# A transformer kernel on Trainium2: ScalarE's and VectorE's order set by hand around the norm ahead of the FFN, transposes over four PSUM banks, eight operand sums moved

## The chip, the cores and the metric

The kernel runs on one core of one Trainium2 chip. The metric is the device time of one execution in microseconds (us). Three runs of the kernel before were timed; the trace is of a further execution, taken with the hardware profiler. TensorE (PE) does matmuls and transposes, ScalarE (ACT) casts and activations, VectorE (DVE) sums and products, GpSimd (POOL) some sums and the stores; SyncE (SP) issues the loads.

## What is computed

Two transformer blocks in a row, on 1024 tokens of width 1024, in float32. The first is attention and a mixture of experts. The second is a gated delta rule and a band attention side by side, an output product with w_out2, and an FFN with a causal convolution. Cut to what stands around the change, with the second block's names:

```python
x = rmsnorm(x1, norm_final)            # end of the first block
x = x + mix @ w_out                    # "w_out2" in the kernel
h = rmsnorm_2(x, norm_ffn_w)           # the norm ahead of the FFN
u = causal_dwconv(h @ w_up, conv_ffn_w) + conv_ffn_b
gate, up = jnp.split(u, 2, axis=-1)
x = x + (jax.nn.silu(gate) * up) @ w_down
```

## The kernel before

**Products in halves.** Every float32 operand of a product is split into a high and a low part (`split`, L53 to L62: a cast on ACT, L59, and a subtraction on VectorE, L62), and a product is three matmuls per k-tile (`acc3`): high by high, high by low, low by high. Names ending in h or hi, and l or lo, are these parts.

**w_out2.** `phase2_wout` computes mix @ w_out2 and adds it to x, which it holds as `xs`, eight row blocks of 128 tokens (they come in by SP's queue and are first multiplied by the first block's norm, L1713). Two halves `hf` of four row blocks each; in each half four loads `n`, each of 256 columns of w_out2. `load` (by `load_w`) brings a load as four pieces: a transfer of 256 KB into a raw tile `waraw`, a cast to `wahi`, a subtraction to `walo`. There are two raw tiles and six pairs wahi and walo. For each of the four row blocks 24 matmuls of 256 columns (8 k-tiles by 3) go to one PSUM bank of two (`pa(0, 2)`, tiles t0 and t1), and VectorE adds the bank to xs (L1779, "the xs sum"). The matmuls' left operands are `mh` and `ml`, parts of mix.

**The posts.** The first four row blocks are complete after half 0. Their norm lies in half 1: behind loads 0 and 1 two `post(t)` each. A post is a Square on ACT with a sum (L1719), the reciprocal root (L69 on VectorE, the root L100 on ACT, L101 to L104 on VectorE), the scaling (L1721) into `XN[t]`, and two `put`s: four transposes on PE (L44) to a bank, then the split into B11 (first 512 columns of the row block) and B21 (the others), the right operands of the FFN's products. `put` takes the banks t2 and t3 in turn (`pa(2, 4)`).

**The last four row blocks** are prepared behind load 2 (`early_post`: a Square of the first half, and L1742, the product of 768 columns with the norm's weights) and finished behind load 3 (`late_post`, L1746 to L1753): the Square of the other half, the product of 256 columns, the root's chain, a scaling on ACT, and two subtractions, L1752 and L1753, which make the operands of the FFN's `t1` and `t2` products: the FFN is done with Strassen-Winograd's seven products per block, and B11, B21, t1, t2, t3, t4 and 22 are their right operands.

**The first two FFN steps.** E holds four pieces of w_up2, loaded and split ahead (`early`, raw tile waraw as well). A loop of four does `prod` (48 matmuls) with E, then puts t1 and t2 of row block i, and then two sums on GpSimd (L1800 and L1801) that make the operands of t3 and t4. `phase2_ffn` then goes on with the pairs j; ahead of its first products it runs `late`, the puts of t3, t4 and 22, one between each two products.

**What sets the order.** PE's order is written out by hand from the last w_out2 load on (`tc.manual_schedule(engines={PE})`, entered at L1771): PE takes its instructions as they are written. Elsewhere, and on the other engines throughout, the framework's scheduler places each instruction on its engine's queue by its own account of when it can start, so that the written order and the queue's order differ. Each engine works its queue in order, and waits by semaphore for the others.

## Time and profile before

| | |
|---|---|
| median of three runs | 2887.88 us (2882.08 to 2892.51) |
| profiled execution | 2887.97 us, span 2886.2 us |
| instructions | 37138 |
| PE busy | 2671.0 us, 93% of the span |
| VectorE busy | 1840.4 us, 64% |
| ACT busy | 1241.2 us, 43% |
| GpSimd busy | 1105.5 us, 38% |
| TensorE's granted clock, mean | 0.965 |

The span runs from the first to the last instruction of the profiled execution. A row of the busy time by stretch says between which two times of the span it lies, how long that is, how long each engine worked in it (and in how many instructions, in brackets), what clock TensorE was granted (PEclk, 1.00 is full speed), what share of the time the DMA engines were busy and what they moved. A row of waits says which instruction waited for which, how long in sum, how often, and the longest. The product with w_out2 begins at about 2075 us, its last load ends near 2181, and from 2240 on only the FFN's products run on PE.

### The profile page before, as it was taken

What the parts mean: (1) busy time and instruction counts of PE and PEld (TensorE: products, weight loads), DVE (VectorE), ACT (ScalarE), POOL (GpSimd) and SP (SyncE); (2) the same over time, 40 slices, a digit from 0 to 9 for tenths busy, and PEclk for the clock granted to TensorE, in tenths of its full rate; (3) what the DMA queues carried; (4) which work ended last, traced back from release to release, by engine and by line L of the source; (5) the groups of instructions that cost most, each with busy time, mean ns of one, the idle gap of its engine ahead of it and who ended that gap; (6) DMA issues with size and microseconds to landing.
All of it is one profiled execution on the core that took longest, in us unless ns stands there. A gap on an engine that the chain in (4) does not pass through costs nothing.

```text
span 2886.2 us, 37138 instructions
## 1 busy us (share of the span) xinstructions
PE 2671.0 (93%) x13916; PEld 2143.9 (74%) x13916; DVE 1840.4 (64%) x2725; ACT 1241.2 (43%) x2032; POOL 1105.5 (38%) x950
## 2 busy tenths in 40 slices
PE   6999998999948999699999899999997999999998
PEld 4786665555836777588889788877896888888886
DVE  3655557784687998756437334375656998886354
ACT  4545554454325676543322223454234444443343
POOL 1103437887344888412121232040004766662000
PEclk8998999999978999899999999999999999999999
DMA  7113310001567999612453544312532122225452
GB/s 226 42 40 122 118 37 1 1 23 34 175 223 246 373 373 370 196 37 88 155 180 111 189 144 139 116 45 88 164 114 103 73 88 82 87 78 200 145 179 99
DMA packets 175956, 382.83 MB, mean 133 GB/s; under 512 B 18664, under 2 KB 84200, under 8 KB 170656
## 3 DMA queue, kind: packets, MB, share of 16 engines
q1 hardware_dynamic: 153056, 298.45, 30.6%
q0 software_dynamic: 22720, 82.02, 8.5%
q8 instruction: 109, 1.79, 0.3%
q14 instruction: 71, 0.58, 0.1%
HBM read 311.19 MB, written 69.22 MB: 132 GB/s over the span
## 4 chain that ended last, share of the span: by engine, by line
PE 50%; DVE 4%; issue 1%; DMA 1%; ACT 1%; POOL 0%; SPq 0%; DVEq 0%; ACTq 0%; POOLq 0%
PE t L41 25%; PE big L41 22%; PE t L44 2%; DVE Rb L1396 1%; DVE bP L1593 0%; DVE Rt L1395 0%; DVE xs L1713 0%; DMA xs<-xacc 0%; ACT bPT L1611 0%; DVE Al L62 0%; DVE mm L1589 0%; DVE walo L62 0%; DMA waraw<-in_w_up 0%; DMA out<-y 0%; DVE rst L102 0%
## 5 line engine op out<-in xcount | busy, mean ns | idle before, releaser
L62 DVE TENSOR_TENSOR mlo<-mraw,mhi 128x2048 fp32r<-128x2048 f32 x63 | 220.2, 3521 | 10.1 <-ACT mhi L59 10.0
L41 PE MATMUL big<-hhi,whi 128*128 128x512 f32 x656 | 210.5, 400 | 0.0
L41 PE MATMUL big<-hlo,whi 128*128 128x512 f32 x656 | 208.5, 396 | 0.0
L41 PE MATMUL big<-hhi,wlo 128*128 128x512 f32 x656 | 207.5, 395 | 0.0
L59 ACT CAST mhi<-mraw 128x2048 fp32r<-128x2048 f32 x96 | 181.5, 1913 | 56.0 <-PE big L41 30.3
L62 DVE TENSOR_TENSOR Al<-raw,Ah 128x512 fp32r<-128x512 f32 x150 | 115.6, 772 | 129.4 <-ACT Ah L59 127.6
L62 POOL TENSOR_TENSOR mlo<-mraw,mhi 128x2048 fp32r<-128x2048 f32 x33 | 164.9, 5002 | 76.0 <-ACT mhi L59 75.4
L59 ACT CAST Ah<-raw 128x512 fp32r<-128x512 f32 x150 | 92.7, 621 | 217.5 <-PE t L41 215.4
L812 POOL TENSOR_TENSOR acc<-acc,P 128x512 f32<-128x512 f32 x128 | 167.9, 1338 | 36.3 <-ACT P L805 35.7
L62 DVE TENSOR_TENSOR wlo<-wraw,whi 128x512 fp32r<-128x512 f32 (+5 forms) x124 | 78.7, 644 | 122.7 <-ACT whi L59 121.2
L805 ACT ACTIVATE P<-t 128x512 f32<-128x512 f32 x160 | 94.6, 597 | 120.2 <-PE t L41 116.6
L41 PEld LDWEIGHTS big<-hlo,whi 128*128 128x128 f32 x656 | 122.8, 189 | 26.3
L41 PEld LDWEIGHTS big<-hhi,wlo 128*128 128x128 f32 x656 | 122.8, 189 | 26.1
L41 PEld LDWEIGHTS big<-hhi,whi 128*128 128x128 f32 x656 | 121.0, 189 | 23.6
L59 ACT CAST whi<-wraw 128x512 fp32r<-128x512 f32 (+5 forms) x124 | 69.8, 573 | 139.9 <-PE big L41 118.1
L1841 DVE SCALAR_TENSOR_TENSOR cacc<-ml,cols,cacc 128x1023 f32<-128x1023 f32 x88 | 124.1, 1411 | 9.1 <-ACT cacc L1839 8.4
L700 DVE TENSOR_REDUCE mm<-big 128x1 f32<-128x640 f32 x128 | 101.7, 815 | 28.6 <-PE big L41 28.2
L62 DVE TENSOR_TENSOR Al<-S,Ah 128x512 fp32r<-128x512 f32 x88 | 118.3, 1347 | 2.6 <-ACT Ah L59 2.4
L41 PE MATMUL t<-whi,hlo 128*128 128x344 f32 (+2 forms) x320 | 107.6, 336 | 2.9 <-DVE hlo L62 2.5
L1897 POOL TENSOR_TENSOR cacc<-cacc 128x1024 f32<-128x1024 f32 x22 | 61.0, 2773 | 126.9 <-ACT Ah L59 123.7
L41 PE MATMUL t<-whi,hhi 128*128 128x344 f32 (+2 forms) x320 | 108.3, 338 | 0.8 <-ACT z L1198 0.3
L41 PE MATMUL t<-mlo,xh 128*128 128x512 f32 x256 | 101.7, 397 | 6.1 <-POOL mlo L62 3.3
(701 smaller groups left out, 7878.2 us busy)
## 6 DMA issues: line engine op xcount, KB each, us to landing
mraw<-in_w_gate SPq DMA_DIRECT2D x32, 1024.0 KB, 14.5
mraw<-in_w_up SPq DMA_DIRECT2D x32, 1024.0 KB, 13.3
mraw<-in_w_down SPq DMA_DIRECT2D x32, 1024.0 KB, 9.5
wmod<-in_w_mod SPq DMA_DIRECT2D x48, 512.0 KB, 6.2
raw<-in_w_up SPq DMA_DIRECT2D x22, 1024.0 KB, 4.8
raw<-in_w_down SPq DMA_DIRECT2D x22, 1024.0 KB, 5.1
wraw<-in_w2a SPq DMA_DIRECT2D x72, 256.0 KB, 2.8
zd<-cacc POOLq DMA_DIRECT2D x22, 512.0 KB, 3.0
```

The costliest lines, as they stand in the source:

```text
L41: self.nc.tensor.matmul(out, lhsT, rhs, start=start, stop=stop)
L44: self.nc.tensor.transpose(out, in_, self.ident[:n, :n])
L59: nc.scalar.copy(hi, src)
L62: (nc.vector if lo_eng == "dve" else nc.gpsimd).tensor_sub(lo, src, hi.bitcast(F32))
L700: nc.vector.reduce_max(r[:, a * 2 + 1 - e:a * 2 + 2 - e], ps.rearrange("p (a b) -> p a b", a=2)[:, :, :320], axis=AX.XY)
L805: nc.scalar.activation(P, ps, AF.Exp, scale=self.sc_mla)
L812: eng.tensor_add(u["acc"][e], u["acc"][e], P)
L1396: nc.vector.reduce_sum(R[:, j, j + 1:], tmp[:, :n * n].rearrange("p (m i) -> p i m", i=n), axis=AX.X)
L1841: nc.vector.scalar_tensor_tensor(t[:, tap:], x[:, :1024 - tap], self.col("conv_f", (2 - tap) * 44 + m), t[:, tap:], op0=ALU.mult, op1=ALU.add)
L1897: nc.gpsimd.tensor_mul(tg, tg, tu)
```

## The change

1. `others`: ACT's and VectorE's order is set by hand too, by a second `manual_schedule`, made beside PE's, entered at the last load of half 1 and left behind the loop of the first four FFN products.
2. `late_post` is cut into `squares(t)`, `scaled(t)` and `sums(t)`, which are written one row block apart: behind row block t's matmuls stand its squares, the scaling of t - 1 and the sums of t - 2. The scaling of row block 7 and the sums of 6 and 7 stand behind the first and second FFN product.
3. `banks`: in the loop of four the puts take the banks t0 to t3 in turn; afterwards t2 and t3 again.
4. The pieces E[1, b] are loaded and split behind the loop's entry, and no longer ahead of load 3's matmuls.
5. The four sums for t3 go from GpSimd to VectorE (`third`), those for t4 stay on GpSimd (`fourth`); both are written ahead of their puts, behind the first weights' sums in `phase2_ffn`.

```diff
--- before.py
+++ after.py
@@ -1722,7 +1722,7 @@
             nc.gpsimd.dma_start(self.xsd[t * 128:(t + 1) * 128, :], xs[t])
 
         def put(op, i, src):
-            ps = self.pa(2, 4)
+            ps = self.pa(*banks[0])
             for f in range(4):
                 self.tp(ps[:, f * 128:(f + 1) * 128], src[:, f * 128:(f + 1) * 128])
             s = slice(i * 128, (i + 1) * 128)
@@ -1734,6 +1734,7 @@
             put("21", t, XN[t][:, 512:])
 
         SS = {}
+        banks = [(2, 4)]
 
         def early_post(t):
 
@@ -1741,16 +1742,21 @@
             nc.scalar.activation(T2[t], xs[t][:, :512], AF.Square, accum_out=SS[t][:, 0:1])
             nc.vector.tensor_mul(XN[t][:, :768], xs[t][:, :768], nm[:, :768])
 
-        def late_post(t):
-            x, y, t2, ss = XN[t], XN[t - 4], T2[t], SS[t]
-            nc.scalar.activation(t2, xs[t][:, 512:], AF.Square, accum_out=ss[:, 1:2])
-            nc.vector.tensor_mul(x[:, 768:], xs[t][:, 768:], nm[:, 768:])
+        def squares(t):
+            nc.vector.tensor_mul(XN[t][:, 768:], xs[t][:, 768:], nm[:, 768:])
+            nc.scalar.activation(T2[t], xs[t][:, 512:], AF.Square, accum_out=SS[t][:, 1:2])
             nc.gpsimd.dma_start(self.xsd[t * 128:(t + 1) * 128, :], xs[t])
+
+        def scaled(t):
+            ss = SS[t]
             nc.vector.tensor_add(ss[:, 0:1], ss[:, 0:1], ss[:, 1:2])
             rs = self.rsqrt(ss[:, 0:1], 1.0 / 1024)
-            nc.scalar.activation(x, x, AF.Copy, scale=rs)
+            nc.scalar.activation(XN[t], XN[t], AF.Copy, scale=rs)
+
+        def sums(t):
+            x, y = XN[t], XN[t - 4]
             nc.vector.tensor_sub(y[:, :512], x[:, :512], y[:, :512])
-            nc.vector.tensor_sub(t2, x[:, 512:], y[:, :512])
+            nc.vector.tensor_sub(T2[t], x[:, 512:], y[:, :512])
 
         def early(j, b):
             raw = wo.tile([128, 512], F32, name="waraw", bufs=2)
@@ -1762,12 +1768,14 @@
         def load(src):
             return self.load_w(wo, src, 256, ks=8, kb=2, tag="wa", rawbufs=2, bufs=6)
         order = self.order = tc.manual_schedule(engines={mybir.EngineType.PE})
+        others = tc.manual_schedule(engines={mybir.EngineType.Activation, mybir.EngineType.DVE})
         for hf in range(2):
             for n in range(4):
                 W = load(I["w_out2"][n])
                 if hf and n == 3:
-                    E = {(j, b): early(j, b) for j in range(2) for b in range(2)}
+                    E = {(0, b): early(0, b) for b in range(2)}
                     order.__enter__()
+                    others.__enter__()
                 for i in range(4):
                     t = hf * 4 + i
                     ps = self.pa(0, 2)
@@ -1780,7 +1788,11 @@
                     if hf and n == 2:
                         early_post(t)
                     if hf and n == 3:
-                        late_post(t)
+                        squares(t)
+                        if i:
+                            scaled(t - 1)
+                        if i > 1:
+                            sums(t - 2)
                 if hf == 1 and n < 2:
                     post(2 * n)
                     post(2 * n + 1)
@@ -1792,22 +1804,38 @@
                 T2 = {4 + i: v[i // 2][:, i % 2 * 512:i % 2 * 512 + 512] for i in range(4)}
         ab = [self.big() for _ in range(2)]
         self.ff0 = [[], []]
+        banks[0] = (0, 4)
         for i in range(4):
             j, b = i // 2, i % 2
+            if i == 0:
+                E.update({(1, b): early(1, b) for b in range(2)})
             self.ff0[j].append(self.prod(ab[j][:, b * 512:(b + 1) * 512], E[j, b], B["21" if b else "11"]))
+            if i == 0:
+                scaled(7)
+                sums(6)
+            if i == 1:
+                sums(7)
             put("t1", i, XN[i][:, :512])
             put("t2", i, T2[4 + i])
-            nc.gpsimd.tensor_sub(XN[4 + i][:, :512], XN[4 + i][:, 512:], XN[4 + i][:, :512])
-            nc.gpsimd.tensor_sub(XN[i][:, 512:], XN[i][:, 512:], T2[4 + i])
+        others.__exit__(None, None, None)
+        banks[0] = (2, 4)
 
         def late(op, slot, srcs):
             v = self.mp.tile([128, 8, 512], F32R, name=slot)
             B[op] = v[:, :4], v[:, 4:]
             for i, src in enumerate(srcs):
                 put(op, i, src)
-        self.late = [lambda: late("t3", "mh1", [XN[4 + i][:, :512] for i in range(4)]),
-                     lambda: late("t4", "ml1", [XN[i][:, 512:] for i in range(4)]),
-                     lambda: late("22", "mh0", [XN[4 + i][:, 512:] for i in range(4)])]
+
+        def third():
+            for i in range(4):
+                nc.vector.tensor_sub(XN[4 + i][:, :512], XN[4 + i][:, 512:], XN[4 + i][:, :512])
+            late("t3", "mh1", [XN[4 + i][:, :512] for i in range(4)])
+
+        def fourth():
+            for i in range(4):
+                nc.gpsimd.tensor_sub(XN[i][:, 512:], XN[i][:, 512:], T2[4 + i])
+            late("t4", "ml1", [XN[i][:, 512:] for i in range(4)])
+        self.late = [third, fourth, lambda: late("22", "mh0", [XN[4 + i][:, 512:] for i in range(4)])]
 
     def phase2_ffn(self):
         nc, tc, I = self.nc, self.tc, self.I
```

In the built program PE's order is the same in both. The other engines' orders differ in the following places. In the rows, xs_17065 to xs_17072 are the row blocks 0 to 7, mh_17604 (before) and mh_17606 (after) is XN[0] to XN[3], ml_17605 and ml_17607 XN[4] to XN[7], t_17607 and t_17609 T2; a t with another number is a PSUM bank.

VectorE in half 0, around the xs sums of load 2, before:

```order
L1779 TENSOR_TENSOR xs_17065<-xs_17065,t_17372 128x256
L62 TENSOR_TENSOR walo<-waraw,wahi 128x512
L1779 TENSOR_TENSOR xs_17066<-xs_17066,t_17398 128x256
L1779 TENSOR_TENSOR xs_17067<-xs_17067,t_17424 128x256
L62 TENSOR_TENSOR walo<-waraw,wahi 128x512 x2
L1779 TENSOR_TENSOR xs_17068<-xs_17068,t_17450 128x256
L62 TENSOR_TENSOR walo<-waraw,wahi 128x512
```

VectorE at the same place in half 0, after:

```order
L62 TENSOR_TENSOR walo<-waraw,wahi 128x512 x4
L1787 TENSOR_TENSOR xs_17065<-xs_17065,t_17374 128x256
L1787 TENSOR_TENSOR xs_17066<-xs_17066,t_17400 128x256
L1787 TENSOR_TENSOR xs_17067<-xs_17067,t_17426 128x256
L1787 TENSOR_TENSOR xs_17068<-xs_17068,t_17452 128x256
L62 TENSOR_TENSOR walo<-waraw,wahi 128x512 x4
```

The four subtractions of a load (L62 on walo), which stood between the xs sums of the load ahead of it, now stand in one piece behind all four of these sums; it is so from load 2 of half 0 on.

VectorE in half 1, behind the last xs sum of half 0, at the first two posts (rsv, rsy and rst are tiles of the reciprocal root), before:

```order
L1779 TENSOR_TENSOR xs_17068<-xs_17068,t_17578 128x256
L69 TENSOR_SCALAR rsv<-ssx 128x1 x2
L1779 TENSOR_TENSOR xs_17069<-xs_17069,t_17632 128x256
L101 RECIPROCAL rsy<-rst 128x1 x2
L102 SCALAR_TENSOR_TENSOR rst<-rsy 128x1 x2
L103 TENSOR_TENSOR rst<-rst,rsv 128x1 x2
L104 SCALAR_TENSOR_TENSOR rsy<-rst,rsy 128x1 x2
L62 TENSOR_TENSOR walo<-waraw,wahi 128x512
L1721 SCALAR_TENSOR_TENSOR mh_17604<-xs_17065,rsy,row_16536 128x1024
L1779 TENSOR_TENSOR xs_17070<-xs_17070,t_17658 128x256
L1721 SCALAR_TENSOR_TENSOR mh_17604<-xs_17066,rsy,row_16536 128x1024
```

VectorE at the same two posts, after, from the last xs sum of half 1's load 0 on:

```order
L1787 TENSOR_TENSOR xs_17072<-xs_17072,t_17712 128x256
L69 TENSOR_SCALAR rsv<-ssx 128x1
L101 RECIPROCAL rsy<-rst 128x1
L102 SCALAR_TENSOR_TENSOR rst<-rsy 128x1
L103 TENSOR_TENSOR rst<-rst,rsv 128x1
L104 SCALAR_TENSOR_TENSOR rsy<-rst,rsy 128x1
L1721 SCALAR_TENSOR_TENSOR mh_17606<-xs_17065,rsy,row_16536 128x1024
L62 TENSOR_TENSOR B11l<-t_17751,B11h 128x4x128
L62 TENSOR_TENSOR B21l<-t_17758,B21h 128x4x128
```

Both roots of a pair of posts stood side by side, ahead of the second xs sum of that load; now the first post stands complete, with its scaling and both splits, behind all four xs sums, and the second post follows it.

VectorE behind the reciprocal roots of the last load, before:

```order
L1752 TENSOR_TENSOR mh_17604<-ml_17605,mh_17604 128x512
L1753 TENSOR_TENSOR t_17607<-ml_17605,mh_17604 128x512
L1752 TENSOR_TENSOR mh_17604<-ml_17605,mh_17604 128x512
L62 TENSOR_TENSOR Bt1l<-t_18342,Bt1h 128x4x128
L1753 TENSOR_TENSOR t_17607<-ml_17605,mh_17604 128x512
L62 TENSOR_TENSOR Bt2l<-t_18349,Bt2h 128x4x128
```

VectorE at the same place, after, behind the root of row block 6:

```order
L1758 TENSOR_TENSOR mh_17606<-ml_17607,mh_17606 128x512
L1759 TENSOR_TENSOR t_17609<-ml_17607,mh_17606 128x512
L1831 TENSOR_TENSOR ml_17607<-ml_17607 128x512
L62 TENSOR_TENSOR Bt1l<-t_18342,Bt1h 128x4x128
L62 TENSOR_TENSOR Bt2l<-t_18349,Bt2h 128x4x128
L1758 TENSOR_TENSOR mh_17606<-ml_17607,mh_17606 128x512
L1759 TENSOR_TENSOR t_17609<-ml_17607,mh_17606 128x512
L62 TENSOR_TENSOR Bt1l<-t_18370,Bt1h 128x4x128
L62 TENSOR_TENSOR Bt2l<-t_18377,Bt2h 128x4x128
```

The sums of the last row blocks (L1752 and L1753, now L1758 and L1759) stand further ahead by a step, and the t3 sums (L1831) stand between the splits of Bt1 and Bt2.

## Rows read from the trace of the kernel before

**Rows 1.** the page, part 1: engine, busy us (share of the span) x instructions.

```profile
PE 2671.0 (93%) x13916; PEld 2143.9 (74%) x13916; DVE 1840.4 (64%) x2725; ACT 1241.2 (43%) x2032; POOL 1105.5 (38%) x950
```

**Rows 2.** busy us by stretch (PE PEld DVE ACT POOL), PEclk, DMA share, GB/s.

```profile
2092.00:2096.00 4.00, 2.56 (x12) 2.56 (x13) 3.61 (x5) 0.62 (x1) 0.00 (x0) 0.61 0.24 67
2104.00:2127.00 23.00, 23.00 (x194) 23.00 (x193) 8.56 (x17) 4.96 (x8) 1.61 (x3) 1.00 0.46 153
...
2140.00:2160.00 20.00, 16.98 (x139) 16.38 (x140) 11.46 (x20) 9.52 (x21) 0.00 (x0) 1.00 0.29 82
...
2181.00:2200.00 19.00, 11.58 (x51) 9.17 (x50) 14.97 (x30) 8.64 (x16) 13.21 (x11) 0.82 0.42 154
...
2240.00:2860.00 620.00, 619.57 (x2732) 512.36 (x2731) 435.46 (x502) 258.16 (x396) 257.47 (x164) 1.00 0.33 117
```

**Rows 3.** waits of PE, 2060 to 2240 us, by releaser: sum, count, longest.

```profile
PE t L44 <- DVE mh L62: 6.9, 2, 5.9
PE t L44 <- DVE Bt1l L62: 6.9, 1, 6.9
PE t L44 <- DVE B11l L62: 3.4, 2, 2.4
PE t L41 <- DVE walo L62: 2.6, 1, 2.6
...
PE t L44 <- DVE Bt2l L62: 0.6, 1, 0.6
```

**Rows 4.** groups by form, 2104 to 2127: xcount, busy, mean ns, idle before.

```profile
L41 PE MATMUL t<-walo,mh 128*128 128x256 f32 x65 | 18.4, 283 | 0.0
...
L62 DVE TENSOR_TENSOR walo<-waraw,wahi 128x512 fp32r<-128x512 f32 x9 | 6.2, 691 | 7.1 <-ACT wahi L59 7.0
L59 ACT CAST wahi<-waraw 128x512 fp32r<-128x512 f32 x8 | 5.0, 620 | 18.0 <-PE t L41 11.0 <-DMA waraw<-in_w_out 6.9
```

**Rows 5.** VectorE's timeline from 2104 us: start, duration, [wait before <- releaser].

```profile
2107.70 0.69 DVE L62 TENSOR_TENSOR walo<-waraw,wahi 128x512 fp32r<-128x512 f32 x1 [3.04 <-ACT wahi L59]
2108.31 0.41 DVE L1779 TENSOR_TENSOR xs<-xs,t 128x256 f32<-128x256 f32 x1
2108.64 0.69 DVE L62 TENSOR_TENSOR walo<-waraw,wahi 128x512 fp32r<-128x512 f32 x1
```

**Rows 6.** PE's timeline after its wait of 2.6 us.

```profile
2094.04 0.41 PE L41 MATMUL t<-wahi,mh 128*128 128x256 f32 x1
2094.25 0.41 PE L41 MATMUL t<-walo,mh 128*128 128x256 f32 x1
```

**Rows 7.** DMA issues, 2085 to 2170 us: xcount, KB each, us to landing.

```profile
waraw<-in_w_out SPq DMA_DIRECT2D x24, 256.0 KB, 3.0
```

**Rows 8.** groups of VectorE by form, 2060 to 2100 us.

```profile
L1713 DVE SCALAR_TENSOR_TENSOR xs<-xs,r,row 128x1024 f32<-128x1024 f32 x8 | 10.1, 1278 | 2.9 <-DMA xs<-xacc 2.9
```

**Rows 9.** VectorE's timeline, 2160 to 2240 us.

```profile
2169.91 0.96 DVE L1742 TENSOR_TENSOR ml<-xs,row 128x768 f32<-128x768 f32 x1
...
2175.59 0.15 DVE L69 TENSOR_SCALAR rsv<-mm 128x1 f32<-128x1 f32 x1
...
2176.59 0.16 DVE L104 SCALAR_TENSOR_TENSOR rsy<-rst,rsy 128x1 f32<-128x1 f32 x1
...
2191.78 1.75 DVE L1752 TENSOR_TENSOR mh<-ml,mh 128x512 f32<-128x512 f32 x1
```

**Rows 10.** groups of VectorE by form, 2127 to 2160 us.

```profile
L1721 DVE SCALAR_TENSOR_TENSOR mh<-xs,rsy,row 128x1024 f32<-128x1024 f32 x4 | 5.1, 1280 | 0.0
```

**Rows 11.** groups of ACT by form, 2127 to 2160 us.

```profile
L1719 ACT ACTIVATE mh<-xs 128x1024 f32<-128x1024 f32 x4 | 4.2, 1049 | 0.7 <-PE t L41 0.7
...
L59 ACT CAST B11h<-t 128x512 fp32r<-128x512 f32 x4 | 2.3, 584 | 1.2 <-PE t L44 1.1
```

**Rows 12.** GpSimd's timeline, 2177 to 2200 us.

```profile
2191.21 1.77 POOL L1800 TENSOR_TENSOR ml<-ml 128x512 f32<-128x512 f32 x1 [2.00 <-DVE mh L1752]
```

**Rows 13.** ACT's timeline, 2160 to 2240 us.

```profile
2212.97 1.85 ACT L59 CAST Ah<-S 128x512 fp32r<-128x512 f32 x3 [2.71 <-POOL S L1851]
```

## The prediction

> **What bounds the kernel now.** I read the page first, then the busy time of each engine by stretch, then PE's waits, then the instructions between. The page shows PE busy for 93% of the span [rows 1]. In the stretch of the FFN's products, from 2240 us on, PE is busy in 619.57 of 620 us [rows 2]: whatever is lost or won before it moves the end by as much. The change touches 2075 to 2240 us, the product with w_out2, the norm and the first two steps of the FFN. There PE loses time at few places [rows 3]: one wait of 2.6 us for a split weight, two (2.4 and 1.0) for the split of a transposed block in the posts of w_out2's second half, one of 6.9 for Bt1l (the wait that the change is about) and one of 5.9 for the split of t3's operand. Between them PE has no idle time at all: in 2104 to 2127 us all 23.00 us are busy [rows 2], and the groups of PE's matmuls there sit idle for 0.0 us [rows 4].
>
> Why PE never waits for weights there is the point of this prediction. A load of w_out2 is four pieces, each a transfer, a cast on ACT and a subtraction on VectorE (walo). There are two raw buffers, so pieces three and four can only be sent for after the first two subtractions of the same load. Before, VectorE takes those of the next load in between the xs sums of the present one: in the trace a walo stands ahead of the sum of 2108.31 and another right behind it [rows 5]. So each load is ready when PE comes to it.
>
> **What the change moves.** The diff says that ACT's and VectorE's order is set by hand from the last load on. The order of the built program says more: from the second load on, VectorE holds four walo, four xs sums, four walo, four xs sums, and the posts stand as they are written (the first two pieces in the part on the change). PE's own order is the same in both. So one must cost not one place but seven loads and two posts. I lay the instructions one after another, each with its duration in the trace.
>
> **A plain load** (half 0, loads 3 and 4, and half 1, load 1). PE ends its last matmul 0.28 us after it starts [rows 4]. Then VectorE does the last xs sum; the subtraction after it starts 0.33 us later (2108.31 to 2108.64) and takes 0.69 [rows 5]. With two hand-overs of about 0.05, PE's second matmul of the load starts 0.28 + 0.04 + 0.33 + 0.69 + 0.05 = 1.39 us after the last of the previous load, where two steps of 0.12 (194 matmuls start in 23 us, [rows 2]) would have been 0.24: 1.15 us lost. The third piece is sent for when that subtraction ends: transfer 3.0 [rows 7], cast 0.62, subtraction 0.69 [rows 4], hand-overs 0.15, together 4.46; PE has twelve matmuls, 1.44 us, until it needs it: 3.0 lost. The fourth follows 0.6 behind the third, which PE's six matmuls of 0.72 cover. Sum 4.1 us, and nothing covers it, since PE is the engine that runs through here. Three loads: **+12.3** (11.4 if the transfers take 2.7).
>
> **Load 2 of half 0** already has the 2.6 us wait. Its third and fourth piece now follow subtractions that stand behind six of the eight first multiplies of xs, 1.28 us each [rows 8], so its last piece comes later: 1.28 + 1.28 more between its pieces and the transfer behind. I take **+3** (0 to +5).
>
> **The two posts of half 1.** The order has, for each of two row blocks: reciprocal root, scaling, two subtractions, then the next block; ACT's order likewise has Square, root, two casts, Square. Before, both roots and scalings ran under the matmuls. After: the last xs sum (0.33), the chain from L69 to L104 (2175.59 to 2176.75, 1.16 [rows 9]), the scaling L1721 1.28 [rows 10] and hand-overs 0.25: PE's transposes start 3.0 us late. Second block: ACT's two casts (0.59 each, the second 0.1 ahead of the first's end), its Square 1.05 [rows 11] and 0.1 until its sum is out (hand-overs are estimates throughout), then the chain 1.16 and 1.28: 4.6, less the four steps of 0.12 of the first block's second transposes: 4.1. Then the next load's first subtraction stands behind B11h, B11l and B21l: 0.59 + 0.69 + 0.69 + 0.69 less 0.5: 2.2; and its third piece is late by 2.5 to 3.0, as above. Together 12 each, 24 for both, less the 2.4 and 1.0 that are waited there now: **+20.5** (17 to 23).
>
> **The last load** pays the 4.1 of a plain one, 0.96 more because its first subtraction stands behind L1742 of row block 7 [rows 9], and some 2 more: both subtractions of the FFN's first weights stand ahead of the first xs sum, and PE's third tile wants that sum's bank. From the load's fourth subtraction to that sum's end it is 4.46 (a piece as above) and 0.74, while PE has some 3.7 us of matmuls: **+7** (5 to 9).
>
> **Tail.** Now VectorE comes late to Bt1l, held by blocked sums (1.75 us at 2191.78 [rows 9] beside GpSimd's sum of 1.77 [rows 12], against 0.69 alone for a sum of this size [rows 4]); PE waits 6.9 us, then 0.6 for Bt2l [rows 3], and then works at the lower level for a while (0.82 granted on average in 2181 to 2200 [rows 2], so 0.18 x 19 = 3.4 us of clock lost, some 2.0 of it while PE worked). In the new order the sums of row blocks 4 and 5 are done under w_out2's last load, four banks let the transposes go ahead, and two operand sums come behind the first products. That takes 6.9 + 0.6 + 2.0 = 9.5 away. What is late next: the fourth block's sums stand ahead of the first Bt1l, so the third transposes wait some 2 us, and the first product of the FFN then waits 1 to 2 us more for Ah, which stands behind all eight casts: **-6** (-9.5 to -3). The four sums for t3, now on VectorE (4 x 0.69), stand between its others; GpSimd loses four of eight sums of 1.28 to 1.77. By the Trainium skill's page "SBUF — State Buffer", section "Who interferes with whom", VectorE's sums of two SBUF inputs and GpSimd's instructions hold one pair of ports in turn, the loser blocked for the whole instruction. The rows above agree (1.75 beside 1.77); were the ports shared, moving the sums would give VectorE nothing back, and the tail would be about -3, the sum 3 higher.
>
> The 5.9 us wait stays. It ends with the split of t3's first blocks, and those stand on ACT behind four casts that wait for GpSimd's sums of the next step (2.7 us on L1851 [rows 13]); that part of ACT's order is unchanged, and the sums wait for splits that come after the last Bt2h in both programs.
>
> **The clock.** After the 2.6 us wait the granted clock was 0.61 in 2092 to 2096 us [rows 2]: the lower level, 1.2 GHz, in which 256-column matmuls follow at 0.21 instead of 0.12 us [rows 6]: 12 of them, 1.1 us lost. After waits of 2.4 and 1.0 us the clock stayed at 1.00 [rows 2, 3]. The new waits are of 1 to 4 us, so some will be followed by such a stretch: two at each post surely, the loads at times. I take six of 1.1: **+6** (0 to +13).
>
> Sum: 12.3 + 3 + 20.5 + 7 - 6 + 6 = 42.8, so **+43 us**. The profiled execution took 2887.97 us (span 2886.2) and the median of three is 2887.88, so no correction: **2931 us**, 1.5% slower.
>
> **Rivals.** (a) *The clock falls at every start.* Each of eleven starts costs its 1.1 to 1.6 and the tail stays slow: +13 instead of +6, and waits hide a little: 2939 to 2943, taken as **2941**. For it: the waits come every 15 us. Against: the 2.4 us wait cost none. The Trainium skill's page "TensorE: Matmul & The Clock Gate", section "HAM oscillation", describes a kernel in which every K-tile waited for its slice and each began at the lower clock; by it this rival would be the result. The trace bears it out for one of the three short waits. (b) *The clock hardly falls and transfers land in 2.7*: -6 and -4: **2920**. (c) *The loads hide after all and the tail decides, faster.* One mechanism: VectorE's new order loses PE nothing, because a load's pieces were cast early enough, and the removed 6.9 us wait with its slow clock is all that is left: 2888 - 9.5 = **2878**. It decides only if the seven loads and two posts together lose under 9.5 us, 1.3 a load with nothing at the posts; the first xs sum and subtraction alone lose 1.15 before any transfer. For it speaks that nothing in the diff names these loads. (d) *The order is as printed, but half the loss is made good*, should both late pieces of each load be sent for in time: the waits on third pieces (3 us in seven loads) go, **2910**.
>
> **How the numbers follow.** Forecast 2931 (2923 to 2937): 0.58. (a) 0.14, (b) 0.15, (d) 0.08, (c) 0.03, no measurable change 0.02 (tail and loads cancelling). The range takes in (a) and (b): 2915 to 2943. About 0.3%, 8.7 us, is what a measurement of this kernel can tell from no change: slower 0.95, same 0.02, faster 0.03.
>
> **What would show it.** In the profile after: PE's waits for walo and wahi in each load, 1.0 and 2 us or more, where now there is 0.0; waits of about 3 and 4 us at the transposes of B11 and B21, released by L1721; xs sums in fours on VectorE; the granted clock below 1.00 in several stretches between 2090 and 2230; PE's wait for Bt1l down to about 2 us; that before the t3 split still near 6; and the stretch of the FFN's products as long as before. I am wrong if PE runs through the loads, or if the products lengthen too.

## The result and the profile after

The changed kernel takes **2938.15 us** (median of 4 runs, 2935.22 to 2939.75), the kernel before, run beside it, 2884.98. The ratio is 1.0183 (95% interval 1.0167 to 1.0199): 53 us or 1.8% slower. The forecast was 2931, its range 2915 to 2943.

The page's first part, and then PE's waits from 2060 to 2300 us (sum, count, longest), which answer to [rows 1] and [rows 3]:

```profile
PE 2697.2 (92%) x13916; PEld 2164.7 (74%) x13916; DVE 1844.8 (63%) x2729; ACT 1242.8 (42%) x2032; POOL 1097.6 (37%) x946
```

```profile
PE t L41 <- ACT wahi L59: 15.5, 10, 3.9
PE t L44 <- DVE mh L1721: 14.6, 4, 4.3
PE t L41 <- DVE walo L62: 8.7, 10, 2.2
PE t L44 <- DVE mh L62: 6.8, 2, 5.8
PE t L41 <- ACT Ah L59: 2.0, 1, 2.0
PE t L44 <- DVE Bt1l L62: 1.8, 1, 1.8
```

PE waits ten times for a cast of w_out2 (wahi) and ten times for its subtraction (walo), where before it waited once; and it waits four times at the posts' transposes for the scaled row block (L1721). The wait for Bt1l is down from 6.9 to 1.8 us, the one for t3's split is still 5.8.

By stretch, as in [rows 2]: the first seven rows lie between the starts of the fourth xs sums of w_out2's loads (loads 1 and 2 of half 0 together, then loads 3 and 4, then the four loads of half 1), the last row is of the FFN's later products.

```profile
2071.60:2104.60 33.00, 28.92 (x194) 27.00 (x192) 18.95 (x24) 4.02 (x7) 0.00 (x0) 0.84 0.42 145
2104.60:2124.30 19.70, 15.62 (x97) 14.50 (x96) 4.29 (x9) 2.47 (x4) 0.00 (x0) 0.83 0.18 54
2124.30:2142.20 17.90, 14.94 (x97) 14.26 (x96) 4.26 (x9) 2.47 (x4) 1.61 (x3) 0.81 0.41 143
2142.20:2160.60 18.40, 13.72 (x96) 13.04 (x95) 4.29 (x9) 3.57 (x5) 0.53 (x1) 0.91 0.31 91
2160.60:2190.30 29.70, 20.27 (x112) 18.41 (x112) 11.11 (x25) 7.12 (x14) 0.00 (x0) 0.66 0.12 36
2190.30:2218.90 28.60, 19.15 (x113) 17.46 (x113) 13.97 (x27) 9.78 (x22) 0.00 (x0) 0.70 0.12 37
2218.90:2238.80 19.90, 13.91 (x97) 13.28 (x96) 9.91 (x27) 6.53 (x14) 1.60 (x3) 0.83 0.43 148
...
2295.00:2915.00 620.00, 619.09 (x2730) 511.92 (x2729) 431.32 (x498) 256.83 (x395) 258.00 (x164) 1.00 0.33 117
```

The column behind GpSimd's, PEclk, is the one to read: below 1.00 in each of the seven stretches of w_out2, 0.66 and 0.70 in the two that hold the posts. In the kernel before it was 1.00 in loads 3 and 4 and at the posts, and within w_out2 lower only behind the one wait of 2.6 us [rows 2, 3]. In the later products PE is busy for 619.09 of 620 us, as before [rows 2].

Read off the timelines, the time between one load's fourth xs sum and the next one's, in us (half 0's loads 1 to 4 are a1 to a4, half 1's b1 to b4):

| | a2 | a3 | a4 | b1 | b2 | b3 | b4 |
|---|---|---|---|---|---|---|---|
| before | 13.1 | 11.5 | 11.5 | 12.5 | 15.1 | 14.6 | 15.2 |
| after | 19.8 | 19.7 | 17.9 | 18.4 | 29.7 | 28.7 | 20.6 |

And the whole, by the starts of w_out2's first matmul (2073.7 before, 2071.6 after) and of the FFN's first product (2180.8 and 2238.8):

| | w_out2 | PE's waits in it | the rest of it | first product to the end |
|---|---|---|---|---|
| before | 107.1 | 8.1 | 98.9 | 705.4 |
| after | 167.2 | 39.8 | 127.4 | 698.6 |

So w_out2 lost 60.2 us, 31.7 in waits and 28.5 in the rest. Counted by PE's steps in it (from the start of one matmul or transpose to the next, waits taken off), some 23 of the 28.5 are work at the lower of PE's two levels, and some 5 are steps right beside a wait, which at the upper level too take about 0.23 us instead of 0.12. The tail gained 6.9; and the time ahead of w_out2, which the change doesn't touch, was 2.1 shorter in this execution. Together 51.2, the difference of the two profiled spans. (That start lies between 2067 and 2079 us in the executions below, so single ones are compared by these two columns.)

One load in close-up, at load a3 of the changed kernel; VectorE first (start, duration, wait before and its releaser):

```profile
2104.59 0.42 DVE L1787 TENSOR_TENSOR xs<-xs,t 128x256 f32<-128x256 f32 x1 [2.46 <-PE t L41]
2104.93 1.29 DVE L62 TENSOR_TENSOR walo<-waraw,wahi 128x512 fp32r<-128x512 f32 x2
2109.03 0.69 DVE L62 TENSOR_TENSOR walo<-waraw,wahi 128x512 fp32r<-128x512 f32 x1 [2.81 <-ACT wahi L59]
```

PE over the same time, its rows with a wait and two of those behind them:

```profile
2105.67 0.39 PE L41 MATMUL t<-walo,mh 128*128 128x256 f32 x1 [1.00 <-DVE walo L62]
...
2109.05 0.38 PE L41 MATMUL t<-wahi,mh 128*128 128x256 f32 x1 [1.80 <-ACT wahi L59]
2109.77 0.38 PE L41 MATMUL t<-walo,mh 128*128 128x256 f32 x1 [0.34 <-DVE walo L62]
...
2111.42 0.58 PE L41 MATMUL t<-wahi,mh 128*128 128x256 f32 x1 [0.80 <-ACT wahi L59]
...
2112.53 0.41 PE L41 MATMUL t<-wahi,ml 128*128 128x256 f32 x1
2112.74 0.41 PE L41 MATMUL t<-wahi,mh 128*128 128x256 f32 x1
```

VectorE takes the last xs sum at 2104.59 and the first two subtractions right behind it; the third can only start at 2109.03, 4.1 us after the first started, since its transfer was sent for when that one had ended. PE stands 1.00 us for walo, then 1.80 for the third piece's cast and 0.80 for the fourth's, and behind the last wait its matmuls follow at 0.21 us, the lower level.

At the first pair of posts (in b2), PE:

```profile
2163.46 1.97 PE L44 MATMUL t<-ident,mh 128*128 128x128 f32 x8 [2.91 <-DVE mh L1721]
2169.77 1.94 PE L44 MATMUL t<-ident,mh 128*128 128x128 f32 x8 [4.34 <-DVE mh L1721]
2172.90 0.58 PE L41 MATMUL t<-wahi,mh 128*128 128x256 f32 x1 [1.19 <-ACT wahi L59]
...
2177.04 0.58 PE L41 MATMUL t<-wahi,mh 128*128 128x256 f32 x1 [0.62 <-ACT wahi L59]
```

The waits of 2.91 and 4.34 us are those of the two scalings; the eight transposes take 1.97 and 1.94 us.

### The profile page after: what moved, and what is told of

Read it like the earlier page. It is cut to its first block, busy times and chain, and to the rows that moved or that the text cites. A ratio compares the mean times of both kernels' runs of the same rounds, so it can differ in the third digit from the quotient of the medians.

```text
span 2937.4 us, 37144 instructions
## 1 busy us (share of the span) xinstructions
PE 2697.2 (92%) x13916; PEld 2164.7 (74%) x13916; DVE 1844.8 (63%) x2729; ACT 1242.8 (42%) x2032; POOL 1097.6 (37%) x946
## 4 chain that ended last, share of the span: by engine, by line
PE 73%; DVE 12%; issue 5%; ACT 4%; DMA 3%; POOL 2%; SPq 0%; DVEq 0%; ACTq 0%; POOLq 0%
PE t L41 40%; PE big L41 29%; PE t L44 4%; DVE mlo L62 2%; DVE mm L700 1%; POOL mlo L62 1%; DMA waraw<-in_w_out 1%; PE big L44 1%; DVE Rb L1396 1%; DVE M L703 1%; DMA wmod<-in_w_mod 1%; DMA xacc<-y,idx 1%; ACT mhi L59 0%; DVE walo L62 0%; DVE iu L980 0%
## 5 line engine op out<-in xcount | busy, mean ns | idle before, releaser
L62 DVE TENSOR_TENSOR mlo<-mraw,mhi 128x2048 fp32r<-128x2048 f32 x63 | 220.2, 3521 | 9.6 <-ACT mhi L59 9.5
L62 DVE TENSOR_TENSOR Al<-raw,Ah 128x512 fp32r<-128x512 f32 x150 | 114.3, 764 | 126.7 <-ACT Ah L59 124.8
L62 POOL TENSOR_TENSOR mlo<-mraw,mhi 128x2048 fp32r<-128x2048 f32 x33 | 165.0, 5006 | 73.9 <-ACT mhi L59 73.4
L62 DVE TENSOR_TENSOR wlo<-wraw,whi 128x512 fp32r<-128x512 f32 (+5 forms) x124 | 80.6, 659 | 124.0 <-ACT whi L59 123.3
L41 PEld LDWEIGHTS big<-hhi,whi 128*128 128x128 f32 x656 | 121.2, 189 | 23.6
L62 DVE TENSOR_TENSOR Al<-S,Ah 128x512 fp32r<-128x512 f32 x88 | 119.6, 1363 | 3.1 <-ACT Ah L59 2.9
L700 DVE TENSOR_REDUCE mm<-big 128x1 f32<-128x640 f32 x128 | 101.8, 815 | 28.6 <-PE big L41 28.0
L41 PE MATMUL t<-wlo,hhi 128*128 128x344 f32 (+2 forms) x320 | 106.9, 334 | 0.0
## 6 DMA issues: line engine op xcount, KB each, us to landing
mraw<-in_w_gate SPq DMA_DIRECT2D x32, 1024.0 KB, 13.3
mraw<-in_w_down SPq DMA_DIRECT2D x32, 1024.0 KB, 11.1
```

What stands on the lines that cost most here:

```text
L41: self.nc.tensor.matmul(out, lhsT, rhs, start=start, stop=stop)
L62: (nc.vector if lo_eng == "dve" else nc.gpsimd).tensor_sub(lo, src, hi.bitcast(F32))
L700: nc.vector.reduce_max(r[:, a * 2 + 1 - e:a * 2 + 2 - e], ps.rearrange("p (a b) -> p a b", a=2)[:, :, :320], axis=AX.XY)
```

## The experiments

Two theories stood at the start. **The order theory**: nearly all of the loss lies in w_out2, from ACT's and VectorE's written order, about half of it in waits and half in the lower clock that follows them. **The parts theory**: some other part of the change (four banks, sums on VectorE, later loads of E) costs it. Each run is told by its edit, against the changed kernel unless it says otherwise.

### Without the hand-set order

```diff
-        others = tc.manual_schedule(engines={mybir.EngineType.Activation, mybir.EngineType.DVE})
...
-                    others.__enter__()
...
-        others.__exit__(None, None, None)
```

> The change without the hand-set order of ACT and VectorE; all its other parts stay (the cut of late_post, four banks, E[1, b] later, t3 sums on VectorE). Order theory (the 53 us come from the written order of ACT and VectorE in w_out2's loads and posts): the stretch from w_out2's first matmul to the FFN's first product goes from 164 us back to 103 or so, PE has no waits in the loads but the 2.6 us one, and the time is 2876 to 2888 us. Rival (another part of the change costs it: the banks, the sums moved to VectorE, or the later E loads): it stays above 2900 us, with the waits somewhere else than in the loads.

Measured: 2883.29 us, ratio to before 0.9986 (0.9974 to 0.9998). w_out2 takes 107.0 us, its stretches are those of before to 0.2 us except b4 (14.1), and PE's waits there are the old ones (the last two of these lines; the first two lie in the tail):

```profile
PE t L44 <- DVE mh L62: 4.7, 2, 3.7
PE t L41 <- ACT Ah L59: 4.2, 1, 4.2
PE t L44 <- DVE B11l L62: 3.4, 2, 2.4
PE t L41 <- DVE walo L62: 2.6, 1, 2.6
```

There is no wait for Bt1l any more, the one for Ah has grown to 4.2 us (1.3 before), and from the first product to the end it takes 699.1 us. So the hand-set order makes the whole loss; and the tail's gain, which the change set the order for, comes without it (698.6 with it, 699.1 without).

### Which engine's order

```diff
-        others = tc.manual_schedule(engines={mybir.EngineType.Activation, mybir.EngineType.DVE})
+        others = tc.manual_schedule(engines={mybir.EngineType.Activation})
```

> The change with the order set by hand on ACT only; VectorE's is the scheduler's. Order theory: in half 0, where ACT has only the casts of the pieces, the loads run through (13, 11.5 and 11.5 us from fourth to fourth xs sum, as before); at the posts ACT's written order (Square, root, two casts, then the next Square) still holds VectorE up, so these keep most of their 15 us: 2900 us (2892 to 2912). Rival (ACT's order is what makes the pieces late): half 0 at 18 to 20 us a load, 2925 us or more.

> The change with the order set by hand on VectorE only; ACT's is the scheduler's. Order theory: VectorE's four subtractions behind four xs sums are what makes the pieces late, so half 0 is as in the change, 18 to 20 us a load; the posts are a little shorter, since both Squares stand early: 2930 us (2922 to 2938). Rival (ACT's order does it): half 0 runs through at 11.5 us a load, 2905 us or less.

Measured: 2902.04 us with ACT's order alone, 2946.5 with VectorE's alone (one execution each). From a2 to b4, in us: ACT alone 13.3, 11.5, 11.5, 11.5, 25.0, 26.1, 13.1; VectorE alone 18.5, 19.1, 17.0, 18.3, 29.7, 30.4, 21.7. The stretch of a3 and a4 together, with ACT's order alone and then with VectorE's alone (as above, PEclk behind GpSimd's column):

```profile
2101.90:2124.90 23.00, 23.00 (x194) 23.00 (x193) 8.61 (x16) 5.08 (x9) 1.61 (x3) 1.00 0.50 156
```

```profile
2110.80:2146.90 36.10, 29.24 (x193) 27.47 (x192) 8.53 (x17) 5.08 (x9) 1.61 (x3) 0.86 0.31 101
```

So the plain loads' loss is VectorE's order and not ACT's. At the posts each engine's order is enough for most of the loss: both hold the two posts of a pair one behind the other. VectorE's alone is 8 us over the change as a whole, outside the expectation, but not in w_out2 (166.8 us against 167.2): that execution started w_out2 7.4 us later.

### The loads written between the sums

`piece(l, p)` loads and splits piece p of load l; its definition is left out here.

```diff
...
+                        if i == 3 and k in (1, 3) and l < 7:
+                            nxt += piece(l + 1, 2 + k // 2)
...
+                    if i in (0, 1) and l < 7:
+                        nxt += piece(l + 1, i)
...
```

> The whole change, with the pieces of each w_out2 load written between the xs sums of the load ahead (first and second piece behind the first two sums, third and fourth inside the fourth row block's matmuls); the posts are written as in the change. Order theory: the loads of half 0 and the first of half 1 run through again (6.8 + 8.2 + 6.4 + 5.9 us come back), the third-piece waits behind the posts and at the last load go too (some 9 us with their clock); the waits of 2.9 and 4.3 us at the transposes of both posts stay: about 2902 us (2895 to 2908). Rival (it is the hand-set order as such, or a clock that falls by itself, not where the pieces stand): 2925 us or more.

Measured: 2898.18 us, 1.0037 (1.0024 to 1.0050). With the hand-set order still there, a2 to b1 take 9.7, 11.5, 11.9 and 11.1 us; what is left are the posts:

```profile
PE t L44 <- DVE mh L1721: 15.8, 4, 4.3
```

```profile
2072.30:2124.00 51.70, 47.93 (x390) 46.92 (x389) 30.02 (x43) 10.21 (x17) 1.61 (x3) 1.00 0.53 174
...
2135.10:2159.90 24.80, 16.30 (x112) 15.73 (x112) 11.27 (x26) 8.58 (x16) 0.00 (x0) 0.79 0.15 42
2159.90:2183.40 23.50, 16.25 (x114) 16.02 (x115) 13.66 (x27) 8.68 (x22) 0.00 (x0) 0.78 0.16 46
```

By stretch, PEclk is 1.00 in half 0, 0.79 and 0.78 in the stretches of the posts (b2 24.7 us, b3 23.6). At the loads it was not that the order is set by hand, but what stands in it.

### Two more raw tiles

In a2 to a4 the third and fourth piece go to a tile that is idle then, so that their transfers need not wait for the first two subtractions.

```diff
...
+            for p in range(2):
+                hi, lo = [wo.tile([128, 2, 256], F32R, name=f"wa{w}", bufs=6) for w in ("hi", "lo")]
+                raw = spare[:, p * 512:(p + 1) * 512].rearrange("p (a n) -> p a n", a=2)
...
```

> The change, with two raw tiles more in half 0's loads 2 to 4 (pieces three and four go to a tile that is idle then), so that their transfers need not wait for the load's first two subtractions. Theory (the third piece waits for a transfer that is sent for too late): at loads 3 and 4 of half 0 the first wait for walo, 1.0 us, stays, the waits for wahi of 1.8 and 0.8 us go, with part of the lower clock behind them; from fourth xs sum to fourth xs sum 13 to 16 us, where it is 19.7 and 17.9 now; 4 to 14 us off the whole. Rival (the pieces are late because ACT's casts or VectorE's subtractions stand late, whatever the transfers do): the waits for wahi stay over 1 us and the stretches near 19.7 and 17.9.

Measured: 2932.18 us (one execution), with w_out2 at 154.0 us against 167.2. Loads a3 and a4:

```profile
2110.07 0.39 PE L41 MATMUL t<-walo,mh 128*128 128x256 f32 x1 [1.00 <-DVE walo L62]
...
2122.86 0.39 PE L41 MATMUL t<-walo,mh 128*128 128x256 f32 x1 [1.00 <-DVE walo L62]
```

```profile
2109.00:2121.80 12.80, 11.80 (x97) 11.58 (x96) 4.11 (x9) 2.48 (x4) 0.00 (x0) 1.00 0.27 84
2121.80:2134.60 12.80, 11.80 (x97) 11.58 (x96) 4.11 (x9) 1.24 (x2) 1.61 (x3) 1.00 0.43 160
```

One wait of 1.00 us a load is left, and 12.8 us from sum to sum: 1.3 more than before, so that the wait costs 0.3 beside itself, at the upper level. The late transfer it was that made the other waits. And the clock: here, behind a single wait of 1.00 us, PEclk is 1.00; in the change, with 1.80 and 0.80 behind the same 1.00, it is 0.83. So of the 6.9 us that load a3 gets back, 2.9 are waits; of the other 4.0, some 3.3 are the lower level, by PE's steps, and some 0.7 steps beside the waits.

### PE kept busy at the posts

```diff
...
             normed(t)
+            fill(18 if t % 2 else 12)
             put("11", t, XN[t][:, :512])
...
```

> The change, with matmuls of 512 columns whose results nobody reads on PE ahead of each post's transposes (12 ahead of the first of a pair, 18 ahead of the second), fewer than fill the waits of 2.9 and 4.3 us. Clock theory (the lower clock is what follows PE's idle times, and half of the loss): eight transposes take about 1.0 us in place of 1.95, the granted clock in the stretch of the posts rises from 0.50 to 0.66 to 0.9 or more, and the row blocks behind them run at 0.12 us a matmul: 2926 to 2932 us. Rival (the clock there does not hang on PE's idle times): the transposes stay at 1.95 us and the time is 2938 us or up to 3 more.

Measured: 2937.79 us, 1.0167 (1.0140 to 1.0194): the time of the rival. But PE at the first pair says more:

```profile
2167.03 1.09 PE L44 MATMUL t<-ident,mh 128*128 128x128 f32 x8 [0.16 <-DVE mh L1721]
...
2172.51 1.07 PE L44 MATMUL t<-ident,mh 128*128 128x128 f32 x8 [0.28 <-DVE mh L1721]
2174.82 0.38 PE L41 MATMUL t<-wahi,mh 128*128 128x256 f32 x1 [1.25 <-ACT wahi L59]
2175.74 0.38 PE L41 MATMUL t<-walo,mh 128*128 128x256 f32 x1 [0.53 <-DVE walo L62]
...
2176.37 0.41 PE L41 MATMUL t<-wahi,ml 128*128 128x256 f32 x1
```

The transposes take 1.09 and 1.07 us in place of 1.97 and 1.94: PE, busy with the added matmuls until just ahead of them, is at the upper level. Then it waits 1.25 and 0.53 us for the next load's pieces, and from 2176.37 its matmuls follow at 0.21. The stretches b2 and b3 are 27.4 and 27.4 us, 2.3 and 1.2 shorter; w_out2 as a whole took 163.1 us, 4.1 less than in the change, in an execution that began it 3.1 us later. So the clock at the transposes does hang on PE's idle times, as the theory had it, but its size was wrong: filling the waits saved the work right behind them, and behind the next unfilled ones the lower level came all the same.

### The posts written apart too, and the first multiplies of xs

On top of the loads written between the sums, each Square now stands one row block ahead, the rest of a norm behind an xs sum, and one put of B11 or B21 behind each row block of b2 and b3; ACT's and VectorE's order is set by hand.

```diff
...
+                    if l == 4 and i < 3 or l == 5 and i == 0:
+                        rest(i if l == 4 else 3)
+                        if l == 4:
+                            square(i + 1)
+                    if l in (5, 6):
+                        j = (l - 5) * 2 + i // 2
+                        put("21" if i % 2 else "11", j, XN[j][:, i % 2 * 512:i % 2 * 512 + 512])
...
```

> The run with the loads' pieces between the xs sums, and the posts of half 1 written apart as well: each Square one row block ahead, the rest of a norm behind an xs sum of load 0 (the fourth behind load 1's first), one put of B11 or B21 behind each row block of loads 1 and 2. ACT's and VectorE's order is still set by hand. Order theory (what is left of the loss are the waits at the posts, 15.8 us, and the lower clock behind them): the stretches from fourth to fourth xs sum of loads 1 and 2 of half 1 go from 24.7 and 23.6 us to 12.5 or less, no wait of PE for L1721's tile is over 1 us: 2873 us (2868 to 2880), faster than before. Rival (VectorE has too much to do in half 1, some 31 of 35 us, and its hand-set order turns that into waits at other places): over 2885 us.

Measured: 2882.73 us, 0.9974 (0.9964 to 0.9985), faster than before. The time lies between the theory's range and the rival's bound: b2 and b3 are 15.5 and 14.7 us, not 12.5, since I had left out that each holds sixteen transposes (13.1 is the shortest b2 of all runs), and the one large wait left is the split of B11, of 2.0 us. PE's waits in w_out2 are 6.2 us in all.

```diff
...
+                    if l == 1:
+                        first(4 + i)
...
```

> As the run with the posts written apart, and the first multiplies of xs (the line that was L1713) of row blocks 4 to 7 written behind the xs sums of half 0's second load, since these blocks are needed in half 1 only. Order theory: PE's waits for xs sums in half 0's first load (1.5 us) go, 1 to 3 us less than that run: 2871 us (2866 to 2879). Rival (the first load waits for the transfers of xs, not for these multiplies): the same time within 1 us.

Measured: 2882.27 us, 0.9972 (0.9961 to 0.9983): the same time, as the rival said. The wait for an xs sum goes (0.4 for 1.8 us), one for a cast of w_out2 grows by 1.0 (2.1 for 1.1), and ACT's cast there waits for its transfer.

And that source with the order left to the scheduler:

```diff
...
-                    others.__enter__()
...
-        others.__exit__(None, None, None)
...
```

> The run with loads, posts and first multiplies written apart (2882 us with the order of ACT and VectorE set by hand), without the hand-set order. Order theory (the written order alone was at fault; a hand-set order as such gains nothing here): within 3 us of 2882. Rival (the hand-set order brings the gain of that run): 2886 us or more.

Measured: it takes **2878.33 us, 0.9956 (0.9941 to 0.9971)**, the fastest of all, and by the medians 3.9 us below the run with it, though the two intervals touch. w_out2 takes 101.8 us here and 105.4 with the order set by hand; PE's waits there are 2.9 and 6.1. Its stretch of w_out2, by engine as above, with PEclk at 1.00:

```profile
2077.70:2179.50 101.80, 98.54 (x801) 95.99 (x800) 65.44 (x123) 35.90 (x70) 4.99 (x8) 1.00 0.46 152
```

So neither of the two expectations: the hand-set order gained nothing here, and in the one traced execution of each it cost 3.6 us of w_out2 against the scheduler's order of the same source.

### Where the tail's gain is from

Against the kernel before, one part each: the banks t0 to t3 in the loop of four, and the t3 sums on VectorE.

```diff
+        banks[0] = (0, 4)
         for i in range(4):
...
-            nc.gpsimd.tensor_sub(XN[4 + i][:, :512], XN[4 + i][:, 512:], XN[4 + i][:, :512])
+                nc.vector.tensor_sub(XN[4 + i][:, :512], XN[4 + i][:, 512:], XN[4 + i][:, :512])
```

> The kernel before with the four banks alone in the loop of the first four FFN products (nothing else of the change). What is asked: which part brings the 6.5 us that the stretch from the FFN's first product to the end is shorter in every run with the change's other parts, with or without a hand-set order (705.4 us before; 698.6 in the change, 699.1 without the hand-set order). Banks theory (the transposes of the second row block wait for a bank, and VectorE's late split of Bt1 counts only for that reason): the 6.9 us wait falls below 3 and the stretch is 699 to 701 us, the whole 2880 to 2884. Sums theory (VectorE comes late to the split, held by GpSimd's sums): the stretch stays above 703 us and the time within 3 us of the kernel before.

> The kernel before with the t3 sums alone on VectorE, written ahead of their puts. Sums theory (VectorE's own sums were stretched beside GpSimd's, 1.75 us in place of 0.69; fewer sums on GpSimd let it come to Bt1l earlier): the 6.9 us wait falls to 2 or 3, the stretch from the first product to the end is 699 to 702 us, the whole 2880 to 2884. Banks theory: the sums take their time on VectorE and the two banks still hold the second row block's transposes: the wait stays over 5 us, the time within 3 us of the kernel before or a little over it.

Measured: 2885.12 us, 0.9987 (0.9977 to 0.9997), and 2884.95, 0.9987 (0.9975 to 0.9999). The wait for Bt1l, 6.9 us before [rows 3], with the banks alone:

```profile
PE t L44 <- DVE Bt1l L62: 2.8, 1, 2.8
```

And with the sums alone:

```profile
PE t L44 <- DVE Bt1l L62: 4.1, 1, 4.1
```

From the first product to the end it is 699.6 us with the banks and 701.6 with the sums (705.4 before, 699.1 with both and the split of late_post). Each part alone takes away a share of one and the same wait (4.1 and 2.8 of 6.9 us), so the gains, 5.8 and 3.8 us, don't add up. The banks' wait and stretch came out as their theory had them, and so did the stretch with the sums, so neither theory rules out the other. VectorE's stretched sum is still there in the changed kernel. VectorE's timeline, two of its t3 sums:

```profile
2239.89 1.77 DVE L1831 TENSOR_TENSOR ml<-ml 128x512 f32<-128x512 f32 x1
...
2244.51 0.68 DVE L1831 TENSOR_TENSOR ml<-ml 128x512 f32<-128x512 f32 x1
```

GpSimd's timeline at both:

```profile
2239.82 1.29 POOL L1836 TENSOR_TENSOR mh<-mh,row 128x512 f32<-128x512 f32 x1 [2.41 <-DVE row L1759]
...
2244.74 1.58 POOL L1836 TENSOR_TENSOR mh<-mh,row 128x512 f32<-128x512 f32 x1 [3.12 <-DVE row L1759]
```

L1831 takes 1.77 us where it starts 0.07 us behind GpSimd's sum of 1.29. Five us later it starts 0.23 ahead of GpSimd's next sum: it takes 0.68, and GpSimd's sum 1.58. So it is the later of the two that is stretched.

### The other wait of the tail

```diff
...
+            t3 = self.late[0]()
+            next(t3)
+            for late in [lambda: t3] + self.late[1:]:
                 next(first)
...
```

> That run with the hand-set order, and the first two puts of t3 ahead of the first pair's first product instead of behind it, so that they stand ahead of the casts of Ah, which wait for GpSimd's sums. If the 4.6 to 5.8 us wait at t3's third put is the split of its first two puts standing behind those casts on ACT, it goes, and the 2 us wait for Ah is in part filled by the two puts: 2876 us (2873 to 2879). Rival (the first product's operand then comes later by as much, since the split of t3 takes ACT and VectorE first): 2880 us or more.

Measured: 2886.10 us, 0.9989 (0.9976 to 1.0002), no gain on the 2882.27 us of the run that it builds on (the first multiplies of xs moved, order set by hand). The 4.6 us wait of that run became two:

```profile
2203.13 1.09 PE L44 MATMUL t<-ident,ml 128*128 128x128 f32 x8 [1.01 <-DVE Bt1l L62]
2205.47 0.50 PE L41 MATMUL t<-Bt2h,Ah 128*128 128x512 f32 x1 [1.25 <-ACT Ah L59]
...
2215.82 1.23 PE L44 MATMUL t<-ident,mh 128*128 128x128 f32 x8 [3.22 <-DVE mh L62]
2220.51 1.94 PE L44 MATMUL t<-ident,mh 128*128 128x128 f32 x8 [3.47 <-DVE ml L62]
```

The first two rows are t3's first puts and the product for which they made room: the wait for Ah is shorter (1.25 for 2.1), but the puts wait 1.01 us themselves. t3's third put, at 2208.82, no longer waits. The last two rows are the puts of t4: the first waits 3.22 us for the split of t3's last blocks (mh L62), where it did not wait, and the third 3.47 for the split of t4's first blocks (ml L62), where it waited 1.1. From the first product to the end it takes 700.0 us against 698.2. So the place on ACT was right, and the wait at t3's third put went as expected, but the wait moved to t4 and the time was not won.

## Why the prediction was right, point by point

**What bounds the kernel** held: PE runs through w_out2 before, each wait there reaches the end, and the later products kept their length.

**The place** was right, and it was not where the diff pointed: seven loads and two pairs of posts, all but the last load ahead of the line at which the order is entered. The run without the hand-set order shows it, and the two runs with one engine each confirm that VectorE's four subtractions behind four sums make the loads late. Why an order entered at the last load changes the scheduler's order of the loads ahead of it, no run asked.

**The plain loads**: 12.3 us forecast for three, 11.4 of waits measured (3.9, 2.8 and 4.6). The parts differ. The first subtraction held: from the last matmul of a2 (2104.27) to the one that needs walo (2105.67) it is 1.40 us, 1.39 forecast, of which the trace calls 1.00 a wait. The third piece cost 1.8 and 0.3 in a3, not 3.0: PE's first matmul with it needs only the cast, and the transfer took 2.7 us (ACT's cast starts at 2108.38, the first subtraction ended at 2105.6); in return the fourth cost 0.8 in a3, where I had it covered.

**Load a2**: +3 of waits forecast; loads a1 and a2 together are 2.5 longer (33.0 against 30.5), but their waits are 0.8 shorter (3.9 against 4.7): all of it is the clock (PEclk 0.84 for 0.94) and the steps beside waits. That the size came out near +3 is luck.

**The posts**: +20.5 of waits forecast, 18.6 less the old 3.4, so +15.3, measured. The two scalings were near (3.0 and 4.1 forecast; 2.91 and 4.34). The third piece behind them was not: 0.62 us, not 2.5 to 3.0. As in the plain load, PE needs only the cast and the transfer is 2.7 us, which makes 1.80 of it in a3; the other 1.2 are covered by twelve matmuls at 0.21 us in place of 0.12. The lower clock hid a wait that I had counted at full clock.

**The last load**: +7 forecast, 5.8 of waits measured (1.99 and 3.85).

**The clock** is the term that failed in size. I took six stretches of 1.1 us, twelve matmuls each, from the single such stretch of before [rows 6]: +6, at most 13. Measured: some 23 us, and some 5 more in the steps beside waits. At each of the seven loads the lower level set in, and it lasted for 15 to 32 matmuls of 256 columns (counted as steps of 0.21 us in PE's timeline), not for twelve; the 32 transposes of the posts stood in it as well. The row from which I sized it stood behind one wait with full work after it; here two to four waits follow one another at each load. At a3 and a4 the run with two raw tiles more shows that without the later waits the lower level does not come. What decides it in general stays open, since other runs show both outcomes behind nearly the same waits. By stretch, twelve us of the run with the loads between the sums, with waits of 1.46, 1.02 and 0.34 us:

```profile
2086.00:2098.00 12.00, 9.76 (x77) 9.36 (x78) 7.45 (x12) 2.48 (x4) 0.00 (x0) 1.00 0.46 128
```

And twelve of the run with the posts written apart, with waits of 1.38, 1.12 and 0.34:

```profile
2088.00:2100.00 12.00, 9.65 (x63) 9.25 (x64) 7.07 (x11) 2.48 (x4) 0.00 (x0) 0.86 0.33 102
```

PEclk is 1.00 in the first and 0.86 in the second. Likewise a lone wait of 2.0 us for B11l is followed by the lower level in that second run (0.83 in 2145 to 2155 us), and one of 2.1 is not in the run with the first multiplies moved (1.00 in 2145 to 2155). What makes the lower level last 15 matmuls at one load and 32 at another was not tried.

That 2931 came within 7 us of 2938 is in part luck: the waits were 11 us fewer than the four terms for loads and posts (31.7 for 42.8), while the clock was some 17 more than its term. Rival (a) had the mechanism and 2941 us, nearer to 2938 than my forecast; but its +13 was too small as well, and it came near by the same luck. The section "HAM oscillation" of the Trainium skill's page "TensorE: Matmul & The Clock Gate", on which rival (a) was named, tells of a kernel in which every K-tile waits some 3 to 5 us for its slice and then begins at the lower clock. The changed kernel agrees in that every load has a part at the lower level, but at a3 no wait is over 1.80 us; and the loads a3 and a4 of the run with two raw tiles more, with a wait of 1.00 us and PEclk at 1.00, do not speak against the section, since their waits are shorter than its own.

**The tail**: -6 forecast, -6.9 measured. Bt1l 1.8 us (some 2 forecast), Ah 2.0 (1 to 2 more than 1.3 forecast: 0.7 more), t3 5.8 (to stay). What the prediction didn't see is that this gain needs no order set by hand. Nor did it count that a t3 sum on VectorE can still be stretched beside GpSimd's (1.77 us once).

Rivals (b), (c) and (d) fell: the clock did fall (though (b)'s transfers of 2.7 us were right), the loads did not hide, and no late piece was sent for in time.

## What to carry to other kernels

An order set by hand on one stretch may come with another order far ahead of it, where a scheduler had woven loads, sums and norms together: compare the built order of both programs engine by engine before asking what the stretch itself gains. Write the next load's pieces between this load's sums and each post apart, and leave the order to the scheduler where it does as well: here that was the fastest of all. And price short waits of TensorE in rows with their sequel: in this change they cost some 23 us of clock beside 31.7 of waiting, while one of 1.00 us alone cost no clock at all; and since nearly the same waits ended at either level in two runs, give the clock a wide range of its own.

## What the runs showed of the hardware

A wait of 1.00 us of PE in each of two loads of 12.8 us left the granted clock at 1.00; over a load with waits of 1.00, 1.80 and 0.80 us within 6 us it was 0.83. This is no rule: three waits of 1.46, 1.02 and 0.34 us left it at 1.00 in one run, and three of 1.38, 1.12 and 0.34 were followed by 0.86 over twelve us in another. Work put into PE's idle times kept TensorE at the upper level (eight transposes 1.09 instead of 1.97 us) only until the next waits, of 1.25 and 0.53 us, and the median time of the kernel did not change (2937.79 us against 2938.15). And a sum on VectorE that starts just behind one on GpSimd took 1.77 us instead of 0.68, one that starts just ahead of it left GpSimd's sum at 1.58 instead of 1.29.
